# Seven block products for the values and the recurrence input, as token rows, in three of four super-blocks of a streaming encoder step

## The chip, the cores and the metric

The kernel runs on one core of one Trainium2 chip. The metric is the device time of one execution in microseconds. Three runs of the kernel before took 1247.1, 1247.99 and 1250.41 us (median 1247.99).

## The reference

One layer of a hybrid encoder for 2048 frames of a new stream (the prompt) and 64 next frames of a running stream (the sample), D_MODEL = 1024. One input projection feeds two groups of heads; their gated outputs share one output projection.

```
aq, ak, av, ag, hq, hf, hi, hg = jnp.split(rms_norm(x, ln_g) @ w_in, SPLITS, axis=-1)   # 8 x 512 columns
o_a = attn(aq, ak, av) * silu(ag)      # 8 heads x 64; a 64-frame chunk sees itself and the 8 chunks before it, plus bias
f = lb + (1 - lb) * sigmoid(hf)        # 4 heads x 128
S_t = diag(f_t) S_{t-1} + (1 - f_t) hi_t^T;  o_t = S_t^T silu(hq)_t
o_b = rms_norm(o, norm_g) * silu(hg)
y = rms_norm(x + concat[o_a, o_b] @ w_out, ln_f_g)
```

Outputs besides y are the newest 512 rows of keys and values of the prompt, those of the sample, and the recurrent states. The two kinds of columns that matter here are `av` (the values, jobs `pv`) and `hi` (the recurrence input, jobs `hi`).

## The kernel before

**Super-blocks.** The 2112 tokens are worked through in four super-blocks (`SUPER`, L37): 512 prompt tokens each, the second with the 64 sample tokens as well. For each, `x_tile` (L543) loads tiles of 128 tokens, normalises them on ScalarE and VectorE and transposes them on TensorE; `x_split` leaves them in SBUF as `xh` and `xl`, two fp32r parts, features on partitions, tokens along the free dimension. The tiles of the next super-block are started eight jobs before the end of the present one, into the same room as soon as that is no longer read.

**Projections.** A job (`JOBS`, L46) makes 128 of the 4096 projected columns for all tokens of the super-block. `project` (L733) runs three passes (weights high x `xh`, high x `xl`, low x `xh`) over 8 tiles of the inner dimension: 24 matmuls of up to 512 tokens into one of two PSUM banks tagged `acc`, with the weights as stationary operand, so that features come out on partitions. The first two jobs of a super-block run in two halves of tokens. Super-block 1, with 576 tokens, runs all its jobs as blocks of 256 and 320. Where a job's result is split on, moved or passed through silu, its `ev_...` function does it on ScalarE and VectorE, and frees the bank.

**Weights.** In the first super-block raw weights come from HBM, are split into two parts by VectorE and GpSimd (`w_split`, L652) and written back to DRAM (`wd`, 1024 KB each); later super-blocks load these (`weights`, L631) through four buffers tagged `w`. All these DMAs are issued by the sync engine SP, whose queue is in order.

**Values and input.** Both are wanted with tokens on partitions. `ev_v` (L953) copies the bank, transposes it on TensorE through a `tr` bank (`to_rows`, L842), and splits it (`split_v`); `ev_i` (L1367) does the same through the `g` bank. Keys and values of 512 tokens go to DRAM (`carry`) for the next super-block's band.

**Attention and recurrence.** `attention` (L1165) works on one pair of heads at a time (one room `kd`, `v`, `q`); `rec_block` (L1446) on one head's block at a time (one token `rec`), with its triangular matrix in one of two tiles `asb`. Their elementwise work is on VectorE, ScalarE and, for a few steps, GpSimd.

**The output projection** follows when all super-blocks are projected. It uses seven block products of 512 x 512 (Strassen's scheme in Winograd's form) per pair of token tiles. Its combined weights are prepared during super-block 2 by `out_weights` (L681), from raw tiles through `xn` rooms to `wod` in DRAM. Its operand slots come into being once the recurrence has left its room, and two of its seven weights take the rooms of the last pair's keys, queries and values.

**Order of the work.** The program is written out by a planner (`Plan`, L52): each piece of work is a Python generator that yields what it waits for (a time on an engine, a token, a condition); costs per instruction model when that is; the generators run in order of modelled time and priority, and the instructions go into the engines' queues in that order. TensorE's main line is the sequence of jobs; attention and recurrence matmuls are slipped in between as they come ready. Every instruction issued through the planner's queues carries line 266 in the profile, so the profile's groups are told apart by tiles.

## Time and profile before

| | us |
|---|---|
| median of 3 runs | 1247.99 |
| lowest, highest run | 1247.1, 1250.41 |
| span of the profiled execution | 1244.9 |
| TensorE busy in it | 1230.1 |
| VectorE busy | 889.3 |
| ScalarE busy | 701.5 |
| GpSimd busy | 372.8 |

DMA moved 273.29 MB in it, 220 GB/s over the span. The span runs from the first to the last instruction; the profiled execution's own span is the base of every sum below. In the groups of instructions, a row gives line, engine and operation, the tiles written and read (`out<-in`), the shapes, the count, and behind the bar busy us and the mean ns of one; behind the second bar stands the time that the engine sat idle before them, and what ended it. In the timeline, a row's columns are start, length, engine, operation and count; matmuls overlap in the pipeline, so the distance from one start to the next says what one costs.

### The profile page before, as it was taken

To read this page: it belongs to the slowest core of one execution; us is meant where nothing else is said; L and a number is where in the kernel's file an instruction comes from. 1 tells how busy PE (TensorE), PEld (TensorE's weight loads), DVE (VectorE), ACT (ScalarE), POOL (GpSimd) and SP (SyncE) were. 2 spreads that over 40 slices of the span, in tenths; PEclk is the share of its full clock that TensorE was granted. 3 is DMA by queue.
4 is the path that set the end of the run, shared out by engine and by line. 5 is a ranking of instruction groups with operands and counts; after the bars stand their busy time and mean duration, and the time that the engine had idled before them with its cause. 6 is when DMAs were issued, how large, how long until landed. Compare 5 with 4: busy or idle time off the path is not lost.

```text
span 1244.9 us, 22078 instructions
## 1 busy us (share of the span) xinstructions
PE 1230.1 (99%) x8068; PEld 1078.4 (87%) x8068; DVE 889.3 (71%) x1863; ACT 701.5 (56%) x1535; POOL 372.8 (30%) x699
## 2 busy tenths in 40 slices
PE   9999999999999999999999999999999999999997
PEld 8788888999999999998888888998888888888786
DVE  7678769776857578586584748683848574787886
ACT  6353556665655557575565657763636455644443
POOL 7757565111120210202543535100101204441110
PEclk9999999999999999999999999999999999999999
DMA  7788698645353553636859595846463656896431
GB/s 295 257 299 298 228 334 330 223 153 183 142 194 137 203 186 145 215 127 239 277 209 333 211 365 213 290 155 213 137 225 116 227 197 269 310 316 201 128 135 68
DMA packets 95406, 273.29 MB, mean 220 GB/s; under 512 B 10369, under 2 KB 43137, under 8 KB 77634
## 3 DMA queue, kind: packets, MB, share of 16 engines
q1 hardware_dynamic: 95154, 271.62, 62.0%
q8 instruction: 64, 1.05, 0.3%
q14 instruction: 44, 0.36, 0.1%
q10 hardware_dynamic: 144, 0.26, 0.1%
HBM read 188.23 MB, written 85.19 MB: 220 GB/s over the span
## 4 chain that ended last, share of the span: by engine, by line
PE 76%; DVE 5%; issue 2%; DMA 2%; ACT 2%; POOL 1%; SPq 0%; DVEq 0%; ACTq 0%; POOLq 0%
PE acc L266 55%; PE g L266 6%; PE tr L266 5%; PE pv L266 5%; PE s L266 5%; DMA wraw<-in_w_in_dram 1%; DVE xn L266 1%; DVE pr L266 1%; POOL w L266 1%; DMA xn<-in_x_prompt_dram 1%; ACT ck L266 0%; DVE q L266 0%; DMA So<-in_state_hgrn_dram 0%; DVE k L266 0%; ACT sig L266 0%
## 5 line engine op out<-in xcount | busy, mean ns | idle before, releaser
L266 PE MATMUL acc<-xh,w 128*128 128x512 f32 (+2 forms) x2688 | 567.2, 349 | 1.5 <-ACT sig L266 0.8
L266 PEld LDWEIGHTS acc<-xh,w 128*128 128x128 f32 x2688 | 434.4, 189 | 52.5 <-DVE gq L266 1.1
L266 PE MATMUL acc<-xl,w 128*128 128x512 f32 (+2 forms) x1344 | 296.2, 350 | 0.0
L266 PEld LDWEIGHTS acc<-xl,w 128*128 128x128 f32 x1344 | 217.2, 189 | 24.8
L266 DVE CUSTOM_DVE_ANT_0 pr<-s,bias 128x640 f32<-128x640 f32 (+5 forms) x144 | 100.8, 704 | 34.1 <-PE s L266 33.6
L266 ACT ACTIVATE pr<-pr,nm 128x640 f32<-128x640 f32 (+4 forms) x132 | 100.6, 763 | 40.6 <-DVE nm L266 39.6
L266 ACT CAST ph<-tr 128x512 fp32r<-128x512 f32 (+3 forms) x176 | 88.2, 507 | 62.4 <-PE tr L266 33.7
L266 POOL TENSOR_TENSOR w<-wraw,w 128x256 fp32r<-128x256 f32 x120 | 105.2, 906 | 54.4 <-issue 22.4
L266 POOL TENSOR_TENSOR mixa<-mixa,sga 128x256 f32<-128x256 f32 (+1 forms) x36 | 28.1, 783 | 308.5 <-DVE mixa L266 267.0
L266 DVE TENSOR_TENSOR ph<-tr,ph 128x512 fp32r<-128x512 f32 (+3 forms) x176 | 100.6, 590 | 8.6 <-ACT ph L266 7.4
L266 PE MATMUL pv<-ph,v 128*128 128x256 f32 (+2 forms) x344 | 95.7, 370 | 0.5 <-DVE ph L266 0.5
L266 PE MATMUL tr<-ident,pr 128*128 128x128 f32 x580 | 90.6, 273 | 0.4 <-DVE sig L266 0.2
L266 PEld LDWEIGHTS tr<-ident,pr 128*128 128x128 f32 x580 | 70.9, 140 | 13.7 <-issue 2.2
L266 ACT ACTIVATE sig<-acc 128x256 f32<-128x256 f32 (+2 forms) x86 | 42.7, 497 | 61.7 <-PE acc L266 61.5
L266 DVE TENSOR_SCALAR pr<-pr,sm 128x640 f32<-128x640 f32 (+4 forms) x132 | 72.9, 552 | 4.7
L266 ACT COPY vT<-acc 128x512 f32<-128x512 f32 (+2 forms) x62 | 31.0, 500 | 75.8 <-PE acc L266 75.7
L266 DVE TENSOR_TENSOR mixa<-mixa,pv 64x256 f32<-64x256 f32 (+1 forms) x144 | 56.9, 395 | 20.6 <-ACT mixa L266 16.4
L266 PEld LDWEIGHTS pv<-ph,v 128*128 128x128 f32 x344 | 58.2, 189 | 7.2 <-DVE ph L266 0.9
L266 ACT ACTIVATE sig<-sig 128x512 f32<-128x512 f32 (+2 forms) x109 | 57.4, 528 | 9.9 <-DVE gk L266 7.1
L266 POOL TENSOR_TENSOR xn<-wraw,xn 128x256 fp32r<-128x256 f32 x48 | 37.1, 792 | 69.5 <-ACT xn L266 69.5
L266 PE MATMUL s<-kd,q 128*128 128x320 f32 (+3 forms) x232 | 56.8, 315 | 0.4
L266 PE MATMUL s<-kd,ql 128*128 128x320 f32 (+3 forms) x232 | 55.5, 309 | 0.0
(314 smaller groups left out, 2041.8 us busy)
## 6 DMA issues: line engine op xcount, KB each, us to landing
w<-wd SPq DMA_DIRECT2D x96, 1024.0 KB, 5.0
wd<-w SPq DMA_DIRECT2D x32, 1024.0 KB, 7.7
wraw<-in_w_in_dram SPq DMA_DIRECT2D x30, 512.0 KB, 5.7
wod<-xn SPq DMA_DIRECT2D x28, 512.0 KB, 5.5
xn<-in_x_prompt_dram SPq DMA_DIRECT2D x23, 512.0 KB, 5.8
bias<-biasd SPq DMA_DIRECT2D x12, 640.0 KB, 7.0
carry<-kd SPq DMA_DIRECT2D x12, 512.0 KB, 6.2
carry<-v SPq DMA_DIRECT2D x12, 512.0 KB, 6.5
```

Source lines behind the costliest of these rows:

```text
L266: r = f(*args, **kw)
```

## The change

The sample's 64 tokens move from super-block 1 to super-block 0. In super-blocks 1 to 3 the 16 jobs `pv` and `hi` of before, without their transposes, are replaced by seven jobs `rv0` to `rv6`: for a pair of 128-token tiles, the [256 tokens x 1024] by [1024 x 1024 (values and input)] product is cut into 2 x 2 blocks and made from seven products. Tokens are the stationary operand and weights the moving one, so rows come out with tokens on partitions. The sums of token blocks are made on VectorE or GpSimd into rooms `rs` or `xn` (`combos`), the results are put together in the rooms of `raw` (`row_sums`), and values (split) and input go to DRAM (`vrow`, `irow`), from where each pair and head loads its part. The combined weights are made once, during super-block 0 (`in_weights`), and kept in DRAM (`wvd`). `out_weights` uses the same new function and waits until the rows of super-block 2 are made. Many recurrence steps may now run on VectorE or GpSimd, whichever the planner finds free (`either2`); one `asb` tile serves all until the output projection. The jobs' order is rewritten. The core of the diff:

```
@@ SUPER, JOBS
-    (0, 512, [(0, 512)], [(0, 256), (256, 256)]),
-    (512, 576, [(0, 256), (256, 320)], [(0, 256), (256, 320)]),
+    (0, 576, [(0, 256), (256, 320)], [(0, 256), (256, 320)]),
+    (512, 512, [(0, 512)], [(0, 256), (256, 256)]),
...
-JOBS = [[(k, g) for g in range(4) for k in ("hf", "hq", "hi", "hg", "pg", "pq", "pk", "pv")] for _ in SUPER]
...
+JOBS = [[(x[:2], int(x[2])) for x in jobs.split()] for jobs in (
+    "hq0 hf0 hi0 hg0 pg0 pq0 pk0 pv0 hf1 hq1 hi1 hg1 pg1 pq1 pk1 hi2 pv1 hg2 hf2 hq2 pg2 pq2 pk2 pv2 "
+    "hf3 hi3 hq3 hg3 pg3 pq3 pk3 pv3",
+    "hq0 hf0 rv0 rv1 rv2 rv3 hg0 rv5 rv4 hf1 pq0 rv6 pg0 hq1 pk0 pg1 pk1 hf2 hg1 pq1 hq2 hg2 pg2 pq2 "
+    "pk2 hf3 pg3 hq3 hg3 pq3 pk3",
+    "hf0 hq0 rv0 rv1 rv2 rv3 hq1 rv5 rv4 rv6 hg0 pq0 pk0 pg0 pq1 hf1 pg1 hg1 hq2 hf2 pk1 hf3 pg2 pq3 "
+    "hg2 pq2 hq3 pk2 pk3 pg3 hg3",
+    "hf0 hq0 rv0 hg0 rv1 rv2 rv3 pq0 rv5 rv4 pk0 hq1 rv6 hg1 pq1 pg1 hf1 hq2 hf2 pk1 pg0 hf3 hq3 hg2 "
+    "pk2 pq2 pg2 hg3 pk3 pq3 pg3",
+)]
@@ weights
+                if isinstance(nt, tuple):
+                    yield lambda: "combined" in have and all(("split", i) in have for i in (8, 9, 10, 11, 24, 25, 26, 27))
                 yield from tk["w"].get()
                 w = w_pair()
-                sp.dma_start(f32(w), wd[nt])
+                if isinstance(nt, tuple):
+                    sp.dma_start(f32(w).rearrange("p a k n -> p (a k n)").rearrange("p (k n) -> p k n", k=4),
+                                 wvd[nt[0]][:, nt[1]])
+                else:
+                    sp.dma_start(f32(w), wd[nt])
@@ combined weights (block_weights, per quarter a of the inner dimension)
+            t1 = yield from either(t, t3, b22, b12, ALU.subtract, one)
+            C.spawn(split(4, t3, t1), 1.9)
+            t = yield from either(t, b12, b12, b11, ALU.subtract, one)
...
+            t2 = yield from either(t, b22, b22, b12, ALU.subtract, one)
+            C.spawn(split(3, b12, t2), 1.9)
...
+            t = yield from either(t2, b21, b21, b22, ALU.subtract, one)
+            C.spawn(split(2, b22, t), 1.9)
+            C.spawn(split(6, b21, t), 1.9)
@@ combined token blocks (combos)
+        yield from give(2, s2, h21, ((add, h22), (sub, h11), (add, l21), (add, l22), (sub, l11)), C.now)
+        yield from give(3, s1, h21, ((add, h22), (add, l21), (add, l22)), C.now)
+        yield lambda: (sb, pr, 2) in used_x
+        yield from give(5, s2, h12, ((sub, f32(s2[:, 0])), (add, l12), (sub, f32(s2[:, 1]))), used_x[sb, pr, 2])
+        yield lambda: (sb, pr, 3) in used_x
+        yield from give(4, s1, h11, ((sub, h21), (add, l11), (sub, l21)), used_x[sb, pr, 3])
@@ project_rows(j, sb, k)
+        ws = []
+        for i in range(2):
+            yield lambda: j + i in w_at
+            yield w_at[j + i][1]
+            ws.append(w_at[j + i][0].rearrange("p a k n -> p (a k n)"))
+        for pr in range(2):
+            yield from tk["acc"].get()
+            acc = acc_ps()
...
+            for kt in range(4):
+                cs = slice(kt * 512, kt * 512 + 512)
+                for i, (x, part) in enumerate(((hi, 0), (lo, 0), (hi, 1))):
+                    mm(acc, x[:, kt], ws[part][:, cs], 512, start=kt == 0 and i == 0, stop=kt == 3 and i == 2)
+                yield None
+            used_x[sb, pr, k] = C.pe()
+            C.spawn(row_sums(sb, k, pr, acc, C.pe()), 0)
+        tk["w"].put(2, C.pe())
@@ row_sums
+        if k == 0:
+            yield "A", t
+            act.copy(u, acc)
...
+        elif k == 5:
...
+            dve.tensor_add(o, w, acc)
...
+            for out, x in ((w, u),) if k in (1, 3) else ((w, w), (u, u)) if k == 4 else ((u, u),):
+                dve.tensor_add(out, x, acc)
@@ pair's room (open_), head's input (rows_in)
+            if sb:
+                yield lambda: row_n.get(("pv", sb), (0, 0.0))[0] == n
+                yield row_n["pv", sb][1]
+                sp.dma_start(f32(d.v[:, 4:8].rearrange("p t s d -> p (t s d)")),
+                             vrow[sb][p].rearrange("p t x -> p (t x)"))
...
+            yield lambda: row_n.get(("hi", sb), (0, 0.0))[0] == SUPER[sb][1] and ifree()
+            yield row_n["hi", sb][1]
+            sp.dma_start(r.iv[:, 0:4], irow[sb][h])
@@ rec_block
+    def either2(t, out, x, y, op, n):
+
+        e = C.pick(t, D=150.0 + 1.042 * n, P=450.0 + 1.2 * n)
+        yield e, t
+        (pool if e == "P" else dve).tensor_tensor(out, x, y, op)
+        return C.pool() if e == "P" else C.dve()
...
-        dve.tensor_mul(q0[:, :bn], q0[:, :bn], qs[:, c])
...
+        td = yield from either2(tq, q0[:, :bn], q0[:, :bn], qs[:, c], ALU.mult, bn)
@@ out_weights
+        yield lambda: ("rows", 2) in have
+        yield from block_weights(load, wod, ("raw", "raw", "rs", "rs", "xn"), room_of, True)
```

More of the change, by code (lines that the diff above doesn't have):

```diff
@@ L547, in x_tile @@
         if here is None:
-            yield from tk["xn"].get()
-            xn = T(px, [P, D], F32, "xn", bufs=XNB)
+            while not (tk["xn"].n or sb > 1 and tk["raw"].n):
+                yield min((tk["xn"], tk["raw"]), key=Tok.when) if sb > 1 else tk["xn"]
+            room = "xn" if tk["xn"].n else "raw"
+            tk[room].take()
+            xn = T(px, [P, D], F32, "xn", bufs=XNB) if room == "xn" else raw_tile().rearrange("p k n -> p (k n)")
             sp.dma_start(xn[:rows], x_rows(sb, c, rows))
@@ L626, in hymba_step @@
     for sb, jobs in enumerate(JOBS):
-        order += [(sb, feature[k] + g) for k, g in jobs]
+        for k, g in jobs:
+            if k == "rv":
+                order += [(sb, (g, part)) for part in range(2)]
+            else:
+                order.append((sb, feature[k] + g))
     w_at = {}
@@ L755, in project, with combine @@
             tk["w"].put(1, C.pe())
+    made_x, used_x = {}, {}
+    def combine(sb):
+        yield lambda: "combined" in have and all(x_ready(sb, 0, x, k) for x in range(2) for k in (0, 4))
+        yield from tk["xn"].get()
+        x = T(px, [P, D], F32, "xn", bufs=XNB)
+        left = [0, 1]
+        for pr in range(2):
+            C.spawn(combos(sb, pr, x[:, pr * 512 : pr * 512 + 512].rearrange("p (k t) -> p k t", k=4), left), 1)
+        yield lambda: not left
+        tk["xn"].put(1, C.now)
@@ L1343, in ev_f @@
             c = slice(off, off + bn)
-            yield lambda: "bounds" in have and front()
+            yield lambda: "lb" in have and front()
             yield from tk["sig"].get()
@@ L2088, in first_x @@
         def first_x():
-            for c in range(4):
-                C.spawn(x_tile(0, c // 2, c * P, (xr0[c], landed["x", c]), gps), 0)
+            for c in range(5):
+                C.spawn(x_tile(0, min(c // 2, 1), c * P, (xr0[c], landed["x", c]), gps), 0)
             yield lambda: x_laid(0, 1, 1)
```

380 lines of the change are left out of this document (268 added, 112 removed).

## The prediction

> **What bounds the kernel now.** I read the page first (busy time, then the chain), then the busy time stage by stage, then who makes TensorE wait, and last the timeline of TensorE at the places that the change touches.
>
> ```profile
> span 1244.9 us, 22078 instructions
> PE 1230.1 (99%) x8068; PEld 1078.4 (87%) x8068; DVE 889.3 (71%) x1863; ACT 701.5 (56%) x1535; POOL 372.8 (30%) x699
> PE 76%; DVE 5%; issue 2%; DMA 2%; ACT 2%; POOL 1%; SPq 0%; DVEq 0%; ACTq 0%; POOLq 0%
> ```
>
> TensorE is busy for all but 14.8 us, and the chain that ended last runs over it. The other engines have room on the average. The stages, cut where the super-blocks change, say whether that holds everywhere (columns: busy us and instructions of each engine, then granted clock, DMA share, GB/s):
>
> ```profile
> core 0: us, PE busy (x) PEld busy (x) DVE busy (x) ACT busy (x) POOL busy (x), PEclk, DMA share, GB/s
> 0.00:216.00 216.00, 211.90 (x1316) 177.64 (x1317) 167.73 (x314) 112.67 (x232) 140.75 (x221) 1.00 0.81 291
> 216.00:556.00 340.00, 337.82 (x2743) 326.35 (x2742) 245.76 (x624) 212.30 (x510) 49.53 (x163) 1.00 0.50 177
> 556.00:812.00 256.00, 255.23 (x1639) 218.40 (x1638) 172.25 (x349) 158.93 (x336) 100.63 (x170) 1.00 0.75 263
> 812.00:1045.00 233.00, 233.00 (x1497) 198.33 (x1496) 150.83 (x321) 125.71 (x246) 29.24 (x71) 1.00 0.51 178
> 1045.00:1245.00 200.00, 192.18 (x881) 157.65 (x879) 152.71 (x258) 91.89 (x213) 52.67 (x75) 1.00 0.61 208
> ```
>
> It does: in the four super-blocks TensorE idles 4.1, 2.2, 0.8 and 0.0 us, at full clock, though DMA and VectorE run at three quarters in some. Only the start and the end lose anything. So a matmul taken away is worth its full issue time, as long as nothing new makes TensorE wait.
>
> **What goes: products.** In super-blocks 1 to 3 the values (512 columns) and the recurrence input (512) were eight jobs of 24 matmuls. Now each pair of 128-token tiles needs seven block products of 4 tiles x 3 passes = 12 matmuls, 24 for both pairs: seven jobs' worth for eight. Super-block 1 also carried the sample as blocks of 256 and 320 columns; that goes to super-block 0, where the same two widths now apply to all jobs, so the sample's cost only moves. Net: 3 x 24 = 72 matmuls of 512 columns less. Their price is read from a stretch with nothing else on TensorE (start, length with overlap, group):
>
> ```profile
> 595.54 1.98 PE L266 MATMUL acc<-xl,w 128*128 128x512 f32 x8
> 597.35 3.79 PE L266 MATMUL acc<-xh,w 128*128 128x512 f32 x16
> 600.98 1.98 PE L266 MATMUL acc<-xl,w 128*128 128x512 f32 x8
> ```
>
> From start to start, 24 matmuls take 5.44 us, 0.227 us each (the listed lengths overlap by some 0.2 us and are not used). 72 x 0.227 = 16.3 us. The same 24 are the length of one product over both pairs.
>
> **What goes: transposes.** Values and input now come out with tokens on partitions, so their turning goes in super-blocks 1 to 3.
>
> ```profile
> L266 PE MATMUL tr<-ident,vT 128*128 128x128 f32 x80 | 12.9, 271 | 0.0
> L266 PE MATMUL g<-ident,vT 128*128 128x128 f32 x64 | 10.4, 274 | 0.5 <-ACT vT L266 0.5
> ...
> 612.62 0.60 PE L266 MATMUL tr<-ident,vT 128*128 128x128 f32 x4
> 612.98 0.70 PE L266 MATMUL acc<-xh,w 128*128 128x512 f32 x2
> 613.52 0.45 PE L266 MATMUL s<-kd,q 128*128 128x320 f32 x2
> ```
>
> Of the 80 in the first row, 64 are values (4 pairs x 4 tiles x 4 super-blocks) and 16 the last keys; of these 64 and of the 64 in the second row three super-blocks' share, 96, goes. Four take 0.36 us, and the two matmuls behind them 0.54 instead of 0.45: 0.45 us for a group of four, 24 groups, 10.8 us. Together 27.1 us of TensorE's time go, and I find nothing added to it: the sums are made by other engines, and the sample's attention is the same work earlier.
>
> **What comes: weights.** A product's weights are two tiles of 1024 KB, used for 5.44 us; a job had one. TensorE frees both at the product's end, and there are four buffers.
>
> ```profile
> w<-wd SPq DMA_DIRECT2D x96, 1024.0 KB, 5.0
> ...
> DMA to landing us min/median/max: 3.9/5.8/11.7
> ...
> 1050.00:1100.00 50.00, 49.50 (x257) 41.74 (x256) 34.85 (x73) 27.39 (x57) 29.20 (x48) 1.00 0.92 344
> ...
> 550.00:600.00 50.00, 36.61 (x181) 1.00 0.57 212
> ```
>
> The last row is the time in which projections held TensorE where super-block 2 begins: 73%, so 5.44 us of a product last 7.4 us on the clock. The highest rate in a 50 us stretch is 344 GB/s, at a share of 0.92: a tile is 3.05 us of transfer. Two tiles behind each other land 3.9 + 3.05 = 7.0 us after their release at best and 5.8 + 3.05 = 8.9 in the middle case. Against 7.4 us the wait is between 0 and 1.5 us. It can come where a product follows a product: four times in super-block 1, five in 2, three in 3, twelve in all; 0 to 18 us. I take 0.5 us each, 6 us: below the middle, since the trace of before shows no TensorE wait for a weight tile even in super-block 2 at a share of 0.75. Over a whole super-block the bytes fit: super-block 3 moved 178 GB/s x 233 us = 41 MB and gets about 9 MB more (six tiles net, rows written and read back), 50 MB in some 224 us, 223 GB/s. Super-block 2 goes from 67 to about 76 MB, 308 GB/s in 247 us, but the preparation of the output weights, which makes its share high, now starts only behind its last product.
>
> The DMA page of the Trainium skill ("DMA: Bandwidth & Descriptors", section Specifications) gives about 358 GB/s as what HBM yields to one core. By it, as an estimate, a product's 2.1 MB take 5.9 us, more than 5.44, which speaks against a run of products; the trace's 344 agrees.
>
> **What comes: sums.** Each pair of tiles in each later super-block takes 14 sums and 4 low parts of 512 elements to form its four combined inputs, plus 4 copies on ScalarE. There are 7 additions from PSUM and one copy per pair to put the products together, and half-width splits of the value rows. Once, during super-block 0, the weight blocks are combined: 32 operations, 4 MB in and 8 MB out. The old evacuations, splits and copies of values and input go.
>
> ```profile
> L266 DVE TENSOR_TENSOR ph<-tr,ph 128x512 fp32r<-128x512 f32 x108 | 72.7, 684 | 5.3 <-ACT ph L266 4.5
> L266 DVE TENSOR_TENSOR k<-k,gk 128x512 f32<-128x512 f32 x24 | 18.8, 782 | 0.7 <-ACT k L266 0.6
> L266 POOL TENSOR_TENSOR xn<-wraw,xn 128x256 fp32r<-128x256 f32 x48 | 37.1, 792 | 69.5 <-ACT xn L266 69.5
> L266 DVE SCALAR_TENSOR_TENSOR xn<-xn,rstd,gin 128x1024 f32<-128x1024 f32 x20 | 26.8, 1342 | 3.1 <-ACT rstd L266 1.8 <-DMA w<-wd 1.2
> ```
>
> Two-input VectorE operations: 108 for inputs, 42 additions, 32 for weights, about 12 full-width equivalents of splits, less about 16 that go: 178 at 0.68 to 0.78 us, 121 to 139 us. Even if all stay on VectorE it goes from 889 to about 1020 us of some 1222, 83%; the code lets GpSimd take them (two halves at 0.79 us) and lets it take recurrence products too. ScalarE gains some 38 us and loses some 28.
>
> Neither engine becomes the bound by its sum; what counts is delay. The combined inputs come behind 2 jobs and 2 products that don't need them, 4 x 5.44 = 21.8 us of TensorE's own work, or 30 us at 73%, against some 16 us of sums for the first two combinations of both pairs: hidden, and if that cover were gone, at most those 16 us per super-block. The PSUM banks are tighter. One was held by 24 matmuls, now by 12: a bank must be emptied within 2.72 us where 5.44 were allowed. An addition is 0.68 us; with one 1.34 us operation queued ahead it is 2.0. Lateness is bounded by 0 and 0.5 us for each of 42, 21 us; since VectorE's queue is kept short by the planner, I take 2 us.
>
> "SBUF — State Buffer" in the Trainium skill (section Who interferes with whom) says that VectorE operations with both inputs in SBUF and GpSimd operations block each other outright. The 782 against 684 ns above agree in kind; by it, moving sums to GpSimd relieves VectorE by less than the count says.
>
> **At the start and the end.** The sample's 256 KB now come ahead of the third weight tile: at most 0.8 us, hidden behind the wider second blocks (48 matmuls of 320 in place of 256). The combining in super-block 0 adds about 10 MB to a stage that has 291 GB/s and that the sample lengthens: no TensorE wait expected. At the end, the last pair's attention gates output weights. Its stretch of before, from the first score to the last product, took 35 us:
>
> ```profile
> 1059.37 0.46 PE L266 MATMUL s<-kd,q 128*128 128x320 f32 x2
> ...
> 1093.89 0.39 PE L266 MATMUL pv<-ph,v 128*128 128x256 f32 x2
> ```
>
> **The sum.** 1244.9 - 16.3 - 10.8 + 6 + 2 = 1225.8 us of span. The median of the runs, 1247.99, lies 3.1 us above this execution's span; 1229 us.
>
> **The rivals.**
> *Nothing waits.* For it: 2.2, 0.8 and 0.0 us of idle time in the stages with the same double buffering. Then 1248 - 27 = 1221.
> *VectorE's queue is late for the banks.* For it: half the time per bank, 13% more VectorE work. 15 to 21 us of waits: 1236 to 1242, near the line of no change, with slips beyond it.
> *The weight stream binds (slower).* Place: the three or four products in a row at the beginning of a super-block. The recurrence and the attention of a new super-block cannot begin before the last products have delivered their rows, so the work that fills TensorE between jobs may be missing just there. Then a product lasts 5.44 and its weights 8.9 us: 3.5 us each, twelve times, 41 us, 1262. It decides from 27.1 / 12 = 2.26 us a product, that is, weights later than 7.7 us with no filler. Against it: in before, super-block 2 begins with its predecessor's attention still running. By the skill's 358 GB/s two tiles alone would give only 0.4 us each, so it takes the landing time, too.
> *Late attention.* Attention starts only when the seventh product is in, about 12 jobs into a super-block rather than 8. Four pairs at 35 us still fit behind it, and what spills fills the next beginning; in the last super-block ten output steps (27 us) can run ahead of it. If it ends 20 us beyond that, about 1245.
>
> **How the numbers follow.** About 0.3% is what a measurement of this kernel can tell from no change: 1244.2 to 1251.7. Forecast (1224 to 1236) 0.5; nothing waits 0.17; late banks 0.16, a quarter of it within 0.3%; late attention 0.06, half of it within; weight stream 0.11, nearly all slower. Faster 0.82, same 0.08, slower 0.1. The range reaches from below the first rival (startup and end may also lose a few us of their idle time) to the end of the second and into the third: 1216 to 1247.
>
> **What would show it.** Right: about 504 matmuls into acc with weights as the moving side, combined inputs or xh as the other; 48 transposes fewer on tr and 48 on g; TensorE busy near 1203 us; idle time of single us at the beginnings of super-blocks 1 to 3, ended by DMA of weights or by VectorE's additions. Wrong: 30 us or more of TensorE idle (the stream, if DMA ends it; the banks, if VectorE or ScalarE does), or a busy time above 1215 us, which would mean that the products cost more than plain matmuls.

## The result and the profile after

Slower: a median of 1282.8 us (4 runs, 1280.9 to 1285.8) against 1248.2 us for the kernel before on the same chip (4 runs), a ratio of 1.0279 with an interval of 1.0265 to 1.0293. That is 34.6 us more, where the forecast was 19 less. The profiled execution spans 1279.2 us. First the same lines of the page as before, now of the changed kernel: span, busy time, engines on the chain that ended last.

```profile
span 1279.2 us, 22328 instructions
PE 1220.2 (95%) x7900; PEld 1060.5 (83%) x7900; DVE 996.6 (78%) x1936; ACT 703.2 (55%) x1531; POOL 531.0 (42%) x908
PE 67%; DVE 11%; POOL 7%; DMA 6%; ACT 4%; issue 3%; SPq 2%; DVEq 0%; POOLq 0%; ACTq 0%
```

168 matrix instructions are gone, exactly the 72 matmuls and 96 transposes of the working. But TensorE now idles 59 us instead of 14.8, and VectorE, GpSimd and DMA have come onto the chain. By stage (cut where the super-blocks change: the first holds the sample now, 317 us instead of 216):

```profile
core 0: us, PE busy (x) PEld busy (x) DVE busy (x) ACT busy (x) POOL busy (x), PEclk, DMA share, GB/s
0.00:317.00 317.00, 297.97 (x2413) 284.93 (x2414) 267.87 (x591) 188.28 (x470) 191.69 (x379) 0.99 0.79 266
317.00:560.00 243.00, 234.78 (x1484) 198.74 (x1483) 175.35 (x346) 128.32 (x257) 60.62 (x108) 1.00 0.64 228
560.00:836.00 276.00, 263.55 (x1684) 224.89 (x1684) 213.69 (x391) 165.82 (x337) 142.97 (x213) 0.99 0.82 290
836.00:1085.00 249.00, 241.79 (x1513) 204.07 (x1512) 191.61 (x365) 133.57 (x264) 76.73 (x132) 1.00 0.66 239
1085.00:1279.00 194.00, 182.08 (x815) 147.87 (x813) 148.07 (x247) 87.21 (x206) 59.01 (x78) 0.98 0.58 195
```

Every stage loses: 19.0, 8.2, 12.5, 7.2 and 11.9 us of idle time. The waits of TensorE by their cause (total us, times, longest):

```profile
PE s L273 <- DVE nm L273: 6.0, 9, 0.9
PE acc L273 <- DVE gq L273: 5.5, 3, 2.9
PE g L273 <- DVE eb L273: 5.3, 7, 1.3
PE tr L273 <- DVE ph L273: 4.8, 4, 3.2
PE acc L273 <- ACT vT L273: 4.2, 1, 4.2
PE acc L273 <- ACT xh L273: 3.4, 3, 2.3
PE acc L273 <- ACT sig L273: 3.4, 2, 2.4
PE acc L273 <- DMA w<-wvd: 2.9, 3, 2.5
```

No single wait stands out, and they are old ones: score statistics (`nm`), probabilities (`ph`), the recurrence's exponentials (`eb`), gates (`gq`, `sig`). The products' weights (`wvd`) end only 2.9 us. The products themselves run at the planned rate. The timeline of TensorE in super-block 1 (start, length, group):

```profile
371.40 2.88 PE L273 MATMUL acc<-w,rs 128*128 128x512 f32 x12
374.12 2.88 PE L273 MATMUL acc<-w,xn 128*128 128x512 f32 x12
376.84 0.84 PE L273 MATMUL acc<-xh,w 128*128 128x512 f32 x3
```

Twelve matmuls take 2.72 us from start to start, 0.227 each. Now the longest stall, where super-block 2 begins (all engines, some lines left out; in brackets the idle time before and what ended it):

```profile
565.82 1.12 PE L273 MATMUL acc<-xh,w 128*128 128x256 f32 x8
...
567.43 1.84 POOL L273 TENSOR_TENSOR xn<-xn,xh 128x256 f32<-128x256 f32 x2
567.73 0.97 DVE L273 TENSOR_TENSOR ql<-vT,q 64x512 fp32r<-64x512 f32 x1
568.71 0.85 DVE L273 CAST q<-q 64x512 fp32r<-64x512 f32 x1
569.24 2.91 POOL L273 TENSOR_TENSOR xn<-xn,xl 128x256 f32<-128x256 f32 x3
569.59 1.10 DVE L273 TENSOR_TENSOR ql<-vT,q 64x512 fp32r<-64x512 f32 x1
570.72 0.84 DVE L273 CAST q<-q 64x512 fp32r<-64x512 f32 x1
570.73 0.37 ACT L273 COPY vT<-acc 128x256 f32<-128x256 f32 x1 [2.55 <-DVE ql L273]
571.15 1.22 PE L273 MATMUL acc<-xh,w 128*128 128x256 f32 x4 [4.21 <-ACT vT L273]
```

VectorE works without a gap on the last pair's queries, GpSimd on token sums (`xn<-xn,xl`). ScalarE cannot empty a bank until a room `vT` is free, and TensorE cannot go on until the bank is empty. And the stall is not paid once. The busy times around it (columns as for the stages; the granted clock is the third from the end):

```profile
566.00:571.20 5.20, 0.99 (x9) 0.78 (x8) 5.03 (x8) 2.55 (x7) 5.20 (x6) 0.97 0.94 335
570.90:574.30 3.40, 3.15 (x14) 3.15 (x15) 3.32 (x4) 2.53 (x7) 3.40 (x4) 0.50 0.21 88
574.40:577.80 3.40, 3.40 (x30) 3.40 (x29) 3.21 (x7) 1.78 (x5) 1.80 (x3) 1.00 0.11 39
```

For 3.4 us after it TensorE runs at a granted clock of 0.50. "TensorE: Matmul & The Clock Gate" in the Trainium skill (Part 1) says that the array drops to half rate when it has been idle for about 3.4 us, and needs as long a busy stretch to come back; these rows agree. Another drop of the same trace, in the last pair's attention, came without such an idle stretch:

```profile
1093.17:1096.58 3.41, 1.60 (x9) 1.06 (x7) 2.41 (x7) 1.64 (x4) 0.00 (x0) 1.00 0.99 408
1096.60:1103.40 6.80, 5.75 (x20) 5.04 (x21) 3.59 (x10) 3.11 (x7) 1.42 (x2) 0.50 0.80 266
```

TensorE was busy for 1.60 of 3.41 us there, no single wait was longer than 1.02 us, and still the clock stood at 0.50 for the 6.8 us behind it. Here the measurement decides: a few short waits close together can be enough.

**A measure for the rest.** Busy time hides slow matmuls, so I take starts: for all matmul records, the distance to the next start, less the full-clock cost of the group (0.227 us for 512 columns, 0.147 for 320, 0.12 for 256, about 0.1 and less for narrower ones). What is left is TensorE time lost, idle or slowed (four runs of the experiments below stand beside: small edits only, sample moved without products, no token sums with half the weight stream, last super-block without products):

| us lost in | before | e6, small edits | e1, sample first | changed | e9, two costs out | e17, last without |
|---|---|---|---|---|---|---|
| 0 to 300 | 7 | 15 | 35 | 30 | 33 | 39 |
| 300 to 550 | 7 | 8 | 1 | 10 | 2 | 14 |
| 550 to 800 | 0 | 5 | 4 | 14 | 9 | 17 |
| 800 to 1000 | 1 | -1 | 1 | 10 | 12 | 5 |
| 1000 to the end | -1 | 0 | 1 | 11 | 11 | 1 |
| all | 14 | 26 | 42 | 75 | 67 | 75 |

From before to after it grows by 61 us; the span grew by 34.3. The difference, 27, is the matmul work that went; it comes out so by the way the measure is made, and that the forecast's price holds is shown by the 0.227 us of the products above. What failed is the price of the waits. A cell of the table is good to some 4 us, a total to some 2 (by the spans, the totals of e6, e1 and e9 should be 24, 40 and 65).

### The profile page after: what moved, and what is told of

Read it like the earlier page. It is cut to its first block, busy times and chain, and to the rows that moved or that the text cites. A ratio compares the mean times of both kernels' runs of the same rounds, so it can differ in the third digit from the quotient of the medians.

```text
span 1279.2 us, 22328 instructions
## 1 busy us (share of the span) xinstructions
PE 1220.2 (95%) x7900; PEld 1060.5 (83%) x7900; DVE 996.6 (78%) x1936; ACT 703.2 (55%) x1531; POOL 531.0 (42%) x908
## 3 DMA queue, kind: packets, MB, share of 16 engines
q8 instruction: 62, 1.02, 0.3%
## 4 chain that ended last, share of the span: by engine, by line
PE 67%; DVE 11%; POOL 7%; DMA 6%; ACT 4%; issue 3%; SPq 2%; DVEq 0%; POOLq 0%; ACTq 0%
PE acc L273 47%; PE g L273 6%; PE tr L273 5%; PE s L273 5%; PE pv L273 4%; DVE pr L273 2%; SPq L273 2%; DVE xn L273 2%; DMA w<-wvd 1%; ACT sig L273 1%; POOL w L273 1%; DMA ck<-in_cache_attn_k_dram 1%; DMA xn<-in_w_in_dram 1%; DVE kd L273 1%; DMA wraw<-in_w_in_dram 1%
## 5 line engine op out<-in xcount | busy, mean ns | idle before, releaser
L273 PE MATMUL acc<-xh,w 128*128 128x512 f32 (+2 forms) x2304 | 468.0, 342 | 16.4 <-ACT vT L273 4.2
L273 PEld LDWEIGHTS acc<-xh,w 128*128 128x128 f32 x2304 | 364.3, 190 | 55.7 <-ACT vT L273 4.4
L273 ACT ACTIVATE pr<-pr,nm 128x640 f32<-128x640 f32 (+3 forms) x132 | 100.5, 762 | 67.8 <-DVE nm L273 67.6
L273 ACT CAST ph<-tr 128x512 fp32r<-128x512 f32 (+2 forms) x176 | 87.1, 507 | 75.4 <-PE tr L273 37.1
L273 DVE TENSOR_TENSOR ph<-tr,ph 128x512 fp32r<-128x512 f32 (+2 forms) x176 | 101.0, 589 | 26.6 <-ACT ph L273 26.0
L273 DVE CUSTOM_DVE_ANT_0 pr<-s,bias 128x640 f32<-128x640 f32 (+4 forms) x144 | 100.6, 703 | 16.3 <-PE s L273 14.8
L273 PE MATMUL pv<-ph,v 128*128 128x512 f32 (+1 forms) x376 | 98.2, 361 | 0.5
L273 DVE TENSOR_SCALAR pr<-pr,sm 128x640 f32<-128x640 f32 (+3 forms) x132 | 86.7, 657 | 4.7
L273 ACT ACTIVATE sig<-sig 128x256 f32<-128x256 f32 (+2 forms) x110 | 57.4, 524 | 11.9 <-DVE gk L273 9.0
L273 PE MATMUL acc<-w,xh 128*128 128x512 f32 x160 | 54.5, 400 | 5.6 <-DVE gq L273 2.9
```

Source lines behind the costliest of these rows:

```text
L273: r = f(*args, **kw)
```

## The experiments

Letters in the expectations: in the first four, theory A is that elementwise work (VectorE above all) is too much where the sample and the products now stand, and B its rival, that the stream of the products' weights makes the loss. From the second group on the products' late weights are C, B is that GpSimd slows VectorE, D that the rows of values and input come late, E that the products take filler from the late part of a super-block. Each kernel is laid out anew by the planner, so any edit also shuffles the instruction queues.

**The first group: which part of the change costs?**

Products out, sample first, the order of jobs as in the kernel before (`e1`; `ROWS` lists the super-blocks that have products):

```
+ROWS = ()
-        if sb:
+        if sb in ROWS:
             C.spawn(rows_in(), 1)
```

> The changed kernel without its block products: values and recurrence input are projected and transposed as before in all super-blocks, only the sample sits in super-block 0 (and recurrence steps may go to GpSimd). Theory A (VectorE, with the weight splits and the sample in one super-block, holds TensorE up in super-block 0): TensorE's work is that of before, 1210 us without waits, and super-block 0 loses 10 to 15 us more than in before: about 1260 us. Theory B (the stream of product weights makes the loss): there are no product weights, so the time is that of before, 1248.

1271.2 us (two runs), ratio 1.0194 [1.0164, 1.0224]: 24 us slower than before without a single product, and beyond the figures of both theories. A whole loss that the working had at nothing.

Weight sums and low parts left out for the input weights, the other differences likewise (`e3`):

```
-            t1 = yield from either(t, t3, b22, b12, ALU.subtract, one)
+            t1 = t
```

> The changed kernel, leaving out the 32 sums and low parts that combine the input weights in super-block 0 on VectorE and GpSimd (copies on ScalarE, loads and stores stay; the combined weights are then not the right numbers). Theory A: super-block 0 gets back 32 x 0.7 to 0.9 us of VectorE's and GpSimd's time, half of it or more seen by TensorE: 1268 to 1273. Theory B: 1283, since no transfer changes.

1290.8 us, 1.0352 [1.0311, 1.0392]: less work for VectorE, and slower than the changed kernel. The combining is not the cost. The likely reading is that a new layout of the queues alone can cost 8 us, so a difference of that size between two runs counts below only where rows of the trace or a second run bear it out.

Token sums left out, every product reads an unsummed block (`e4`):

```
-            if k in (0, 1, 6):
+            if True:
+                c, k0 = {0: (0, 0), 1: (0, 4), 6: (P, 4), 2: (P, 0), 3: (0, 0), 4: (0, 4), 5: (P, 4)}[k]
```

> The changed kernel, leaving out the sums that form the combined token blocks in super-blocks 1 to 3 (the products read plain blocks of xh and xl instead; the number of matmuls, their weights and the additions from PSUM stay). Theory A: VectorE loses 108 operations just where it is full, at the beginnings of super-blocks 1 to 3, where some 25 us of the loss lie: about 1260. Theory B: products wait for the same weight transfers, 1283.

1281.7 us, 1.0279 [1.0235, 1.0323]: nothing gained, against A. But the profile of this run shows what stepped in, in its first row of TensorE's waits:

```profile
PE acc L273 <- DMA w<-wvd: 9.3, 6, 2.4
```

With the sums gone, the products start earlier and wait for weights, 9.3 us instead of 2.9.

Products in super-blocks 2 and 3 only, sample in super-block 1 as before (`e5`):

```
+ROWS = [2, 3]
-            if sb == 0:
+            if sb == 1:
                 C.spawn(in_weights(), 3)
```

> Block products in super-blocks 2 and 3 alone; the sample stays in super-block 1 as in the kernel before, whose job order super-blocks 0 and 1 keep; all seven weight combinations are made during super-block 1 on GpSimd, where it was 15% busy. TensorE's work falls by 48 x 0.227 + 16 x 0.45 = 18 us against before. Theory A: super-block 0 is as in before, super-blocks 2 and 3 keep their losses of 17 and 9 us, with some loss in super-block 1: about 1250 to 1258. Theory B: ten products' and more waits stay, two thirds of the loss of 61: about 1270.

1288.4 us, 1.0332 [1.0295, 1.0369]. Not usable as it stands: the first product of super-block 2 takes the rooms `raw`, which the sample's cache holds until its attention is over, and TensorE idled for 15 of the 50 us from 560 to 610. e14 gives the cache other rooms.

**The second group: small edits, engines, weights, order.**

No products, sample in its old place, small edits kept (`e6`):

```
-    (0, 576, [(0, 256), (256, 320)], [(0, 256), (256, 320)]),
-    (512, 512, [(0, 512)], [(0, 256), (256, 256)]),
+    (0, 512, [(0, 512)], [(0, 256), (256, 256)]),
+    (512, 576, [(0, 256), (256, 320)], [(0, 256), (256, 320)]),
...
+ROWS = ()
```

> This kernel has the changed kernel's small edits (one score tile instead of two, the recurrence's elementwise steps free to go to GpSimd) but neither of its two large ones: no block products, and the sample stays in super-block 1. If the loss that the run with the sample first showed comes from having the sample's rows in the first stage: within 3 us of the kernel before, 1244 to 1250 us. If it comes from the small edits: 1260 to 1275 us.

1253.4 us, 1.0053 [1.0038, 1.0068]. In between: the small edits cost 6.6 us, and the sample's move the rest of e1's loss, 1.41% or 17.6 us (the two intervals leave 12 to 23). The first stage of e1 and the first two of e6 (before's are in the prediction):

```profile
0.00:300.00 300.00, 281.07 (x2261) 266.69 (x2262) 232.92 (x527) 164.92 (x415) 168.13 (x353) 0.99 0.68 233
```

```profile
0.00:216.00 216.00, 209.54 (x1242) 173.65 (x1243) 163.75 (x301) 113.61 (x236) 155.44 (x239) 1.00 0.74 274
216.00:556.00 340.00, 336.35 (x2763) 323.08 (x2763) 233.71 (x578) 204.06 (x491) 70.40 (x214) 1.00 0.53 186
```

TensorE idles 18.9 us in the first 300 us of e1, and 10.1 us in the first 556 of e6. With the sample in super-block 1, its many small operations meet a GpSimd that is busy for 70 of 340 us; in super-block 0 they meet 168 of 300 us of it, with the weights' splitting. By cause, TensorE's waits in the first 556 us are in e1 9.3 us for the recurrence's operands (`g`), 3.0 for weights being split and 2.9 for the sample's cache from DRAM; in e6 they are 5.3, 0 and 0. Which of these the move made, and through which engine, is read from these rows and not tested.

Recurrence steps all on VectorE (`e2`):

```
-        e = C.pick(t, D=150.0 + 1.042 * n, P=450.0 + 1.2 * n)
+        e = "D"
```

> As the changed kernel, but all steps of the recurrence that may go to either engine are put on VectorE. Theory A (VectorE is too full where the products run and in the first stage): its queue gets longer, 1285 to 1305 us. Theory B (VectorE's instructions are slow because GpSimd works beside them): shorter, 1265 to 1278 us. Theory C (the products' weights arrive late): unchanged within 4 us of 1283.

1305.6 us, 1.0471 [1.0447, 1.0495]: A's sign, just above its range. More work on VectorE costs 23 us, and B's shorter time did not come; that GpSimd slows VectorE is true all the same, as e10 shows.

Half the weight stream (`e7`):

```
+                if isinstance(nt, tuple) and nt[1]:
+                    w_at[j] = w_at[j - 1]
+                    continue
```

> As the changed kernel, but each product fetches only one of its two 1024 KB weight tiles and uses it for both parts, so that the second part of the weights is wrong: 21 MB less to fetch, and four products instead of two ahead. Theory C (weights late): 1255 to 1268 us. Theories A and B: within 4 us of 1283.

1288.3 us, 1.0328 [1.0313, 1.0344]: not faster, but 6 us slower. The DMA rows say that the stream did get lighter (count, KB, median us from issue to landing; the changed kernel, then this one):

```profile
w<-wvd SPq DMA_DIRECT2D x42, 1024.0 KB, 7.1
```

```profile
w<-wvd SPq DMA_DIRECT2D x21, 1024.0 KB, 5.3
```

So the weights alone are not the bound; the prediction's slower rival falls as it was told there.

Products spread, super-block 3 alike, 2 as far as the rooms allow (`e8`; the beginning of super-block 1's order):

```
+JOBS[1] = [(x[:2], int(x[2])) for x in 'hq0 hf0 rv0 hg0 rv1 pq0 rv2 pg0 rv3 pk0 rv5 rv4 hf1 rv6 hq1 pg1 ...
```

> As the changed kernel, with the seven products of a super-block spread between the ordinary projections instead of four in a row, as far as the rooms allow. Theory A: the elementwise work of the products is spread over a longer stretch, 1268 to 1278 us, unless the values and the recurrence input, which come later, push attention and recurrence together further on (then 1283 or more). Theory C: fewer waits for weights too, 1265 to 1275 us. Theory B: unchanged.

1302.9 us, 1.0445 [1.0427, 1.0462]: 20 us worse than in a run. That fits the second half of A's line, or D.

**The third group: two costs at once, and lateness.**

No token sums and half the stream (`e9`): the edits of e4 and e7 together.

> As the changed kernel, with two things left out at once: the token sums (the products read the unsummed rows) and half of the products' weight stream (one tile for both parts), so values and recurrence input are wrong. If each cost covers the other, so that leaving out one alone shows nothing: 1258 to 1270 us. If neither matters (theory D: the values and the recurrence input come late, and their consumers bunch): 1278 to 1290 us.

1267.5 us, 1.0155 [1.0138, 1.0172]: 15.5 us below the changed kernel, where one alone gave nothing and the other 6 us more. The two cover each other: whichever is taken away, the other comes last. In e4 the weights' waits grew to 9.3 us; in e9 no wait of TensorE ends with them. Where the time is won is shown by the turns to super-blocks 1, 2 and 3, in the changed kernel and in e9 (columns as for the stages):

```profile
300.00:350.00 50.00, 43.85 (x280) 38.85 (x278) 42.89 (x99) 28.34 (x69) 21.29 (x35) 1.00 0.58 198
550.00:600.00 50.00, 43.28 (x288) 39.07 (x287) 44.56 (x80) 31.93 (x69) 23.57 (x37) 0.97 0.49 174
800.00:850.00 50.00, 44.85 (x320) 40.88 (x319) 45.36 (x84) 37.70 (x83) 26.54 (x32) 1.00 0.64 211
```

```profile
300.00:350.00 50.00, 50.00 (x333) 45.83 (x333) 39.19 (x108) 30.86 (x78) 13.71 (x27) 1.00 0.54 181
550.00:600.00 50.00, 46.63 (x297) 42.15 (x297) 40.61 (x85) 30.73 (x69) 10.08 (x20) 0.97 0.55 185
800.00:850.00 50.00, 43.74 (x290) 38.24 (x289) 40.66 (x78) 36.01 (x81) 15.36 (x28) 1.00 0.63 231
```

TensorE's idle time goes from 6.2, 6.7 and 5.2 us to 0.0, 3.4 and 6.3: all is won back at the first turn, half at the second, nothing at the third. (The table of lost time shows 8 us between the two kernels and not 15.5, since e9's profiled execution is 3.5 us above its median and the changed kernel's 1.9 below.)

All token sums on GpSimd (`e10`):

```
-                t = yield from either(t, a, x, y, op)
+                t = yield from either(t, a, x, y, op, 'P')
```

> As the changed kernel, with every token sum on GpSimd instead of the engine that the planner picks. Theory A (VectorE's queue at the start of a super-block): 1268 to 1278 us. If the sums' lateness or GpSimd's disturbance of VectorE counts for more: 1285 to 1310 us. Theory D: within 4 us of 1283.

1295.3 us, 1.0380 [1.0349, 1.0411], in the second range. VectorE's relief buys nothing: GpSimd takes 1.8 us for a sum in its two halves (the timeline above) where VectorE takes 0.7, and VectorE is slower beside it. That shows on an operation that is in all kernels 132 times (before, changed, this one; busy us, mean ns):

```profile
L266 DVE TENSOR_SCALAR pr<-pr,sm 128x640 f32<-128x640 f32 (+4 forms) x132 | 72.9, 552 | 4.7
```

```profile
L273 DVE TENSOR_SCALAR pr<-pr,sm 128x640 f32<-128x640 f32 (+3 forms) x132 | 86.7, 657 | 4.7
```

```profile
L273 DVE TENSOR_SCALAR pr<-pr,sm 128x640 f32<-128x640 f32 (+3 forms) x132 | 90.9, 689 | 4.7
```

Its 128x640 form, told apart by what runs beside it, takes 554 ns in the changed kernel where no GpSimd instruction overlaps it (56 times) and 927 where one does throughout (27 times); in before 554 (83 times) and 913 (7 times). `ph<-tr,ph` (128x512), which takes one input from PSUM, lasts 683 ns either way. Each instruction held against the median of its own form with nothing beside it, this slowing is an estimated 47 us of VectorE's time in before and 107 in the changed kernel. By this estimate some 60 us of VectorE's extra load, while its busy time grew by 107, are not more operations but slower ones beside a busier GpSimd.

Rows not awaited (`e11`; the values likewise):

```
-            yield lambda: row_n.get(("hi", sb), (0, 0.0))[0] == SUPER[sb][1] and ifree()
-            yield row_n["hi", sb][1]
-            sp.dma_start(r.iv[:, 0:4], irow[sb][h])
+            yield lambda: ifree()
+            sp.dma_start(r.iv[:, 0:4].rearrange("p t d -> p (t d)"), w_in[h][:, :512])
```

> As the changed kernel, with all products computed and their rows written, but attention and recurrence read other rows that are there from the start (the values of the super-block before, and input weights in place of the recurrence input), so outputs are wrong. Theory D (the rows come late, and what waits for them bunches): 1258 to 1272 us. Theory A: 1278 to 1288 us, since VectorE has the same work in the same stretch.

1300.7 us, 1.0429 [1.0408, 1.0449]: 19 us slower, above both ranges, so D falls. A reading that fits, but was not tested, is that attention and recurrence that may start earlier push their elementwise work into the stretch in which the products already need it.

Free order on top of that (`e12`): e11 with a product after every two projections in super-blocks 1 and 3.

> As the run in which the rows are not awaited, and the products of super-blocks 1 and 3, for which nothing waits now, are spread evenly: one after every two ordinary projections. Super-block 2 as in the changed kernel. Theory A (too much elementwise work in one stretch): 1250 to 1265 us, and the lost time at the starts of super-blocks 1 and 3 gone. If the products lose time wherever they stand: within 5 us of the run in which the rows are not awaited.

1310.2 us, 1.0500 [1.0485, 1.0516], the slowest, against A's forecast: spreading doesn't help even where nothing waits for the products. Its mean granted clock is 0.975, against 0.994 in the changed kernel and 0.999 before: 2.5% of 1309 us, an estimated 33 us at most, go to TensorE at reduced clock after many stalls, the longest of 6.6 us (a bank that waits for `vT`, as above).

**The fourth group: what is left.**

Casts of weights on ScalarE (`e13`):

```
-            dve.tensor_copy(w[:, 0], raw)
+            act.copy(w[:, 0], raw)
```

> As the changed kernel, but the 25 to 29 casts of weight tiles in super-block 0 (0.7 us each on VectorE, 20 us in all) are done by ScalarE. Theory A, that VectorE is full in the first stage once the sample is there: 1268 to 1277 us, and the first 300 us lose 15 to 22 us of TensorE time instead of 30. If the first stage's waits come from the sample's longer chains (its cache, its recurrence blocks) and not from VectorE's load: within 4 us of 1283.

1290.7 us, 1.0350 [1.0325, 1.0376], slower by 8 us and in neither range; the first 300 us lose 40 by the measure above. So the run gives no sign that VectorE's load as a sum makes the first stage slow. That the casts come later on ScalarE, and the weights with them, would fit, but was not tested.

Two super-blocks of products with other rooms (`e14`, here against e5; `vc` likewise, and the combining takes `raw` for `rs`):

```
-        kc = T(px, [P, 2, 512], F32R, "wraw", bufs=RAWB)
+        kc = T(pg, [P, 2, 512], F32R, "rs", bufs=2)
```

> The sample stays in super-block 1, products in super-blocks 2 and 3 only, the weights' combining on GpSimd in super-block 1, as in the earlier run of two blocks; new is that the sample's cache takes other rooms, so that the first products need not wait for the sample's attention. If the sample's move and the wait for rooms were what made the product version slow: 1240 to 1250 us. If the products lose some 10 us in each super-block wherever the sample is: 1253 to 1266 us.

1274.2 us, 1.0214 [1.0191, 1.0237]. The conflict only moved: now a token sum waits for the room `rs` of the sample's cache. TensorE's timeline and the granted clock right after it:

```profile
601.57 5.39 PE L277 MATMUL acc<-w,rs 128*128 128x512 f32 x12 [8.25 <-ACT rs L277]
606.81 0.40 PE L277 MATMUL acc<-w,xn 128*128 128x512 f32 x1
```

```profile
602.00:607.00 5.00, 5.00 (x13) 3.78 (x13) 2.32 (x4) 0.62 (x1) 0.00 (x0) 0.56 0.00 0
```

The wait of 8.25 us is followed by twelve matmuls in 5.24 us instead of 2.72: 10.8 us that are this run's own. Without them it would stand near 1263, still 10 us above e6 with 18 us less TensorE work: an estimated 28 us lost in two super-blocks of products, with the sample where it was before: 14 for each super-block, where 9 are saved.

Short row additions (`e15`): e9, and 32 of 512 columns added.

```
-                dve.tensor_add(out, x, acc)
+                c = slice(0, 512 if k == 1 else 32)
+                dve.tensor_add(out[:, c], x[:, c], acc[:, c])
```

> As the run without the token sums and with half the weight stream, and besides the products' row additions are cut to 32 of 512 columns (the first one of each pair stays whole, one becomes a ScalarE copy), so values and recurrence input are wrong: about 30 additions of 0.6 to 0.7 us less on VectorE, and the PSUM banks come free sooner. Theory A or late banks: 1250 to 1260 us. If what is left lies elsewhere (the smaller edits, the sample, the end): within 4 us of 1267.

1268.1 us, 1.0165 [1.0138, 1.0193], as e9: with the two other costs out, the quick turn of the products' banks is not what costs. The second rival falls as far as it rests on the products' additions. The banks of ordinary projections are another matter: the waits for those in the changed kernel (`acc` ended by `gq`, `vT` and `sig` in the list above) are 13.1 us, and no run takes them away.

**The fifth group: the place of the products.**

Last super-block without products (`e17`; in it the order of jobs of the kernel before, and `wd` written beside `wvd`), last two without (`e18`, `ROWS = [1]`):

```
+ROWS = [1, 2]
...
             have.add(("split", nt))
-            return
```

> As the changed kernel, but super-block 3 projects its values and recurrence input feature by feature, in the order of the kernel before, so that these projections stand between the last attention steps again; 24 matmuls and 8 groups of transposes more, 9 us of TensorE work. Theory E (what is taken out of the late part of a super-block was the filler that kept TensorE busy while attention and recurrence were in their chains): 1268 to 1278 us, and the 13 us lost between 1000 and 1150 us are gone. If the end's loss has another cause: 1283 to 1293 us.

> As the run before it, with products in super-block 1 alone; 18 us more of TensorE work than the changed kernel. If each super-block of products loses about as much as it saves: 1268 to 1276 us, near the 1271 us of the run with the sample first and no products. If the losses come with the sample's move and the end alone: 1283 or more.

e17: 1292.6 us, 1.0355 [1.0329, 1.0380]. e18: 1288.5 us, 1.0321 [1.0304, 1.0338], in its second range (its 8012 matrix instructions are all there, but its outputs y are wrong, for a reason that was not found). The totals speak against E, the place for it. The last projection and the last product of attention, in before, changed and e17 (before's second row is in the prediction, at 1093.89):

```profile
1061.92 0.63 PE L266 MATMUL acc<-xh,w 128*128 128x512 f32 x2
```

```profile
1085.44 0.39 PE L273 MATMUL acc<-xh,w 128*128 128x512 f32 x1
...
1131.21 0.40 PE L273 MATMUL pv<-ph,v 128*128 128x256 f32 x2
```

```profile
1104.42 0.39 PE L275 MATMUL acc<-xh,w 128*128 128x512 f32 x1
...
1137.92 0.39 PE L275 MATMUL pv<-ph,v 128*128 128x256 f32 x2
```

Attention runs on for 32.0 us behind the last projection in before, 45.8 in the changed kernel, 33.5 in e17. From the last projection to the end of the span it is 183.0, 193.8 and 184.5 us. So some 9 us at the end are the products' of super-block 3, and they go with them; at 9 us of saved work that super-block gains nothing. e17 loses as much as the changed kernel all the same: behind 800 us it wins 15, but it loses 70 before them against 54. It writes eight weight tiles twice there, and all queues are laid out anew; which of the two counts was not tested.

The place of the losses follows the place of the products. By the measure of lost time e18 loses as much as e1 from 800 us on, and e14 as much as e6 up to 550, each within 1 us. Behind the turn to super-block 1 e18, with products there, and e1, without, look like this:

```profile
300.00:400.00 100.00, 90.37 (x576) 76.70 (x575) 72.84 (x158) 41.34 (x96) 28.24 (x47) 0.95 0.68 240
```

```profile
300.00:400.00 100.00, 99.77 (x657) 87.96 (x656) 69.68 (x166) 60.46 (x132) 14.32 (x33) 1.00 0.50 179
```

The sizes do not add up, though: e18 is 17 us slower than e1 with 9 us less TensorE work, so one super-block of products loses 26 us there, where three lose 38 in the changed kernel.

Small edits without GpSimd's share (`e19`): e6 with the edit of e2.

> As the run with the small edits alone (no products, sample in super-block 1, 1253 us), but the recurrence's steps that may go to either engine all stay on VectorE, as in the kernel before; what is left of the small edits is the single score tile and the shared rooms. If the steps given to GpSimd are what the small edits cost: 1246 to 1250 us. If it is the single score tile (the next batch of scores must wait until the one before it is read): 1252 to 1256 us.

1250.4 us, 1.0028 [1.0019, 1.0038]: between the two ranges. By the ratios about 3 of the 6.6 us go with the steps given to GpSimd, and 3.5 stay with the single score tile and the shared rooms; a new layout alone can do as much, so neither part is shown.

## Why the prediction was wrong

By ratios, the 34.8 us are: small edits 6.6, the sample's move 17.6 (12 to 23 by the intervals), products 10.6 (5 to 16). The products save 27.1, so their waits cost some 38: 15.5 token sums and weights, each hidden behind the other (e9), 9 at the end (e17), and 13 that no run settled. These are differences along one path of runs; e18 shows that they change with the layout. The prediction's "I find nothing added to it" is what the two failed steps below have in common.

- *TensorE saves 27.1 us.* Right: 168 instructions, and the products run at the 0.227 us a matmul of the working.
- *"The sample's cost only moves."* This step failed, for 17.6 us. The matmuls moved, but their cover did not move with them. That the move costs is shown by e1 against e6. What makes super-block 0 the worse place is argued from its rows only (the recurrence's operands, the splitting of weights, the sample's cache): moving casts off VectorE (e13) did not help.
- *"The combining in super-block 0 ... no TensorE wait expected."* The combining is indeed cheap (e3: not faster without; 0 to 300 us lose 35 without it and 30 with it). The wait came with the sample: e1 has no combining and loses 35 there.
- *Weights 6 us, banks 2 us.* This is the second failed step: 8 us set down, and the sums at nothing, where some 38 came. The term for the products' own banks was small, as taken, where e15 tests it. The weights alone are worth nothing (e7), the sums alone nothing (e4), both 15.5. The working held each cost by itself against TensorE's own work; it never asked what two costs at the same place do together.
- *"If that cover were gone, at most those 16 us per super-block"* for the sums: 15.5 us came in all three super-blocks, with the weights, so that bound held.
- *The recurrence on either engine* was told as a relief and not costed; it is one (e2: 23 us worse without it in the changed kernel), but gave no gain where there are no products (e19: 3 us faster without it, too little to be told from a new layout).
- *Rivals.* "The weight stream binds" had the right side, but alone it is not the mechanism. "Late attention" was right in kind: 13.8 us later, 9 us of time. "VectorE's queue is late for the banks" was right for the banks of ordinary projections (13.1 us of waits), not for the products' own. A rival in which waits of many kinds grow a little in all stages at once was missing, and with it the clock: 0.994 of 1279.2 us is an estimated 7.7 us at most.
- *What would show it.* "30 us or more of TensorE idle" came, ended by VectorE and ScalarE, which the text would have read as late banks; of the some 50 us that the view of waits lists in all, these banks are 13.1. Busy time of 1220 against 1203 does not mean that the products cost more than plain matmuls: their starts are at plan. The slow stretches lengthen it by up to 7.7 us; the rest was not traced.
- *"the trace's 344 agrees"*, of the 358 GB/s that the prediction takes from the Trainium skill: 344 is the highest of the 50 us stretches, but of the 40 slices on the profile's page (31 and 32 us each) one moved 365 GB/s in before and one 396 in the changed kernel, so 358 is not a ceiling in these traces.

Open: the 13 us, which by e9's rows stand at the turns to super-blocks 2 and 3. The trace shows the stall at `vT` (4.2 us and the slow 3.4 behind it) and VectorE without a gap; a third `vT` room would test it, and no run has one. How much of VectorE's lateness is GpSimd's slowing of it, and not the number of its operations, is open too: e2 and e10 move work between the two and never take it from both.

## What to carry to other kernels

In a kernel at 99% TensorE, saved matmuls are worth their price only if what replaces them adds no waits; none of the arrangements tried here (in a run, spread, in one, two or three super-blocks) brought the 27 us. Ask it for each stage, and for two hidden costs together, since each may be the other's cover. A step that is moved takes its work along but not its cover: price it again at the new place. A stall of a few us on TensorE is to be counted with the slow stretch behind it.

## What the runs showed of the hardware that was not expected

TensorE's granted clock stood at 0.50 for 3.4 us after a stall of 4.2 us, and for 6.8 us after a stretch of 3.4 us in which TensorE was busy for 1.60 us and no single wait was over 1.02 us. Not every such stretch is followed by a drop: from 349.0 to 352.4 us of the changed kernel TensorE was busy for 1.42 of 3.40 us, with most of one wait of 3.19 us in it, and the clock stayed at 1.00. Behind the wait of 8.25 us in e14 a group of twelve matmuls took 5.24 instead of 2.72 us. Over the runs the mean clock goes with the time: 0.999 for before, e6 and e19, 0.998 for e1, 0.990 to 0.994 for the changed kernel, e4, e7, e9, e14, e15 and e18, 0.975 to 0.987 for e2, e3, e5, e8, e10 to e13 and e17.

A VectorE operation on SBUF alone (`pr<-pr,sm`, 128x640) lasted 554 ns by itself and 927 with GpSimd beside it throughout; one with an input in PSUM (`ph<-tr,ph`) lasted 683 either way. "SBUF — State Buffer" in the Trainium skill (Who interferes with whom), by which the prediction took GpSimd's relief to be worth less than its count, was used there for operations with both inputs in SBUF. `k<-k,gk` (128x512) is one of them and agrees: 679 ns with nothing beside it in before (2 times), 922 with GpSimd throughout (10 times), 1408 in the changed kernel (7 times). e10 agrees as well: the sums moved to GpSimd brought no gain.
